# A decoder block on one core: first-pass weights as one array, row sums by products with ones, and four places reordered

## The chip, the core and the metric

The kernel runs on one core of a Trainium2 chip. TensorE (PE, with its weight loads as PEld) multiplies matrices into PSUM, VectorE (DVE), ScalarE (ACT) and GpSimd (POOL) work element by element, and SyncE (SP) issues most of the transfers. The metric is the device time of one execution in microseconds; the median of the runs is compared. Everything is computed in float32, or in float32 split into two rounded parts.

## The reference

The block works on 16 learned meta tokens followed by 1024 tokens of width 1024. Its parts, cut to what matters here:

```python
def mixer(xn, w_in, conv_a_w, conv_b_w, conv_b_bias, ln_b_gain, ln_b_bias, w_out):
    h = jnp.einsum("btd,de->bte", xn, w_in)
    b_gate, c_gate, h_a, glu_val, glu_gate = jnp.split(h, [...], axis=-1)
    y_a = b_gate * causal_depthwise_conv(c_gate * h_a, conv_a_w)
    g = glu_val * jax.nn.sigmoid(glu_gate)
    z = causal_depthwise_conv(g, conv_b_w) + conv_b_bias
    y_b = jax.nn.silu(layer_norm(z, ln_b_gain, ln_b_bias))
    return jnp.einsum("bte,ed->btd", jnp.concatenate([y_a, y_b], axis=-1), w_out)
...
h = jnp.concatenate([meta, x], axis=1)
h = h + rms_norm(mixer(rms_norm(h, pre_mix_norm), ...), post_mix_norm)
ff = swiglu(rms_norm(h, pre_ffn_norm), w_gate, w_up, w_down)
h = h + rms_norm(ff, post_ffn_norm)
return h[:, N_META:, :]
```

`rms_norm` divides by the root of the mean square of a token's row; `layer_norm` also subtracts the mean. The input projection has five groups of 512 columns: b, c, h (for the short convolution) and v, g (for the long one of 31 taps).

## The kernel before, in words

**Split products.** A float32 operand is held as a rounded high part and a low part (the rest). `mm3` (L106) then makes three products for one: high by high (L108), high by the other's low (L109), low by the other's high (L110). So every matrix operand costs a rounding on ACT and a subtraction on DVE or POOL before PE can use it.

**Order.** The program is written under a manual schedule: each engine runs its instructions in the order of the code, and an instruction that waits holds up all behind it on its engine. SP and ACT also issue transfers in that order.

**First pass (L194 to L291).** The input comes transposed, 128 features by 1040 tokens for each of eight k, the tokens cut into thirds of 348. The projection is done in units of 128 columns. Three units start together: (g,0) and (v,0) in all three thirds and (g,1) in the first third. Their weights come in pieces: `cut` (L195) splits each unit's 1024 columns into k = 0, k = 1 and 2, and the rest, so nine loads (`load_first`, L205) and nine splits (`split_first`, L208). `round_x` and `rest_x` (L182, L185) scale x by the gain of the norm, which sits in the parameter array `pr`, and split it. The norm's factor itself is put in later, as its value is known only once all of x is there: `square_x` on ACT and `add_x` on DVE sum the squares over k into `sa[0]`. At L86 to L88 six products of the identity with itself warm TensorE up; the identity is made on POOL.

**Row sums (L287 to L315).** The sum over the partitions is taken with nine narrow products, each with 128 tokens of `sa[0]` as the stationary operand and one column of `ones` (value 1/512) as the moving one (L291). The result is a small array with tokens on partitions, of which `rsqrt_n` (L119) takes the inverse root with one step of refinement. `spread_x` (L309) brings it back to one row per token on all partitions by transposes with the identity (L312) and copies into `rB`. The transposes stand between the products of unit 0, at its k = 2, 4 and 6 (`AT`, L530). `start_g` (L505) then uses `rB`.

**Units (L532 to L547).** 18 units follow, each with eight k. The accumulators come from the pool `ps1`, two tiles of three banks by turns (banks 2 to 4 and 5 to 7); the pool `aux` has banks 0 and 1. In each round the next unit's weights are split (`split_unit`, L151: ACT, then POOL, or DVE for the first), the one after is loaded, the last unit's result is worked on (`after`), and taps of the long convolution run on DVE (L372) and ACT with POOL (L358, L359). Layer norm's sums are taken within units 14 and 15: `ln_mean` (L459), `ln_var` (L472: eight narrow products) and `ln_spread` (L481: eight transposes).

**Output projection (L565 to L842).** `group` (L797) takes three, three and two blocks of 128 tokens; `OUT_BANKS` names the pairs of PSUM banks of a group's blocks. `scale_gains` (L501) multiplies two gain vectors by -0.5 on ACT.

**FFN up and gate (L844 to L1033).** The products are done with a Winograd form of Strassen's scheme on two by two blocks: for each of 11 column pairs j and both matrices m there are seven products n, numbered 1, 2, 6, 5, 7, 3, 4, each of four k. Their x side (`X[n]`: B11, B21, T2, T1, T3, B22, T4) is made once; the weight side (`a_side`, L882) is made two steps ahead: sums on DVE, rounding on ACT (L660), subtraction on DVE (L647). Step s runs over `order` (L877), which takes pairs 0 and 1 by turns and then one pair at a time. In step s come the products, then `leave` of step s-1 (L735), extra work, `a_side(s + 2)` and `split`. After a pair's last product `sums` (L782) makes four more blocks out of its result, on POOL; `split` (L771) rounds a block and writes both parts to DRAM for the down projection. `free` (L638) is the queue of PSUM banks.

**FFN down (from L1035)** runs to the end of the span and is not touched.

Of the kernel before, what the change touches and what calls it, by code (L numbers as in the profile page):

```python
# [36 lines left out]
O_MIX = 0  # L37
O_CA = O_MIX + KD
# [8 lines left out]
FILL = 40  # L47
# [8 lines left out]
def hybrid_block(ctx: ExitStack, tc: tile.TileContext, xT, x, w_in, w_out, w_gate, w_up, w_down, par, g_post, g_ffn, g_out, out):  # L56
# [17 lines left out]
    ya = ExitStack()  # L74
    yap = ya.enter_context(tc.tile_pool(name="yap", bufs=8, side="right"))
# [9 lines left out]
    make_identity(nc, ident)  # L85
    pw = aux.tile([P, 512], F32, tag="a", name="warm")  # L86
    for i in range(6):
        nc.tensor.matmul(pw[:, :P], ident, ident, start=True, stop=True)  # L88

    ones = const.tile([P, P], F32, name="ones")  # L90
    nc.vector.memset(ones, 1.0 / 512.0)
    par_ = const.tile([P, lines(NPAR)], F32, name="pr")
# [42 lines left out]
    nc.scalar.dma_start(pr, par)  # L135
# [15 lines left out]
    def split_unit(u, eng=None):  # L151
        wh, wl = (wp.tile([P, D], F32R, tag=t, name=f"{t}_{u[0]}{u[1]}") for t in ("wh", "wl"))
        nc.scalar.copy(wh, raw_w[u])
        (eng or nc.gpsimd).tensor_tensor(wl, raw_w[u], wh.bitcast(F32), op=ALU.subtract)
        split_w[u] = wh, wl
# [26 lines left out]
    def round_x(k, c=slice(None)):  # L182
        nc.scalar.activation(xh[k][:, PAD:][:, c], xs[k][:, c], AF.Copy, scale=pr[:, O_MIX + k : O_MIX + k + 1])

    def rest_x(k, c=slice(None)):  # L185
        nc.vector.scalar_tensor_tensor(xl[k][:, PAD:][:, c], xs[k][:, c], pr[:, O_MIX + k : O_MIX + k + 1], xh[k][:, PAD:][:, c].bitcast(F32), op0=ALU.mult, op1=ALU.subtract)
# [8 lines left out]
    cut = [slice(0, P), slice(P, 3 * P), slice(3 * P, D)]  # L195
    first = {}
    FIRST = [("g", 0), ("v", 0), ("g", 1)]
    for u in FIRST:
        n = f"{u[0]}{u[1]}"
        ws = wp.tile([P, D], F32, tag="ws", name=f"ws_{n}")  # L200
        wh, wl = (wp.tile([P, D], F32R, tag=t, name=f"{t}_{n}") for t in ("wh", "wl"))
        first[u] = ws, wh, wl
        split_w[u] = wh, wl

    def load_first(u, c, eng=None):  # L205
        (eng or nc.sync).dma_start(first[u][0][:, c], w_in[BASE[u[0]] + u[1]][:, c])

    def split_first(u, c):  # L208
        ws, wh, wl = first[u]
        nc.scalar.copy(wh[:, c], ws[:, c])  # L210
        nc.vector.tensor_tensor(wl[:, c], ws[:, c], wh[:, c].bitcast(F32), op=ALU.subtract)

    xs[0] = load_x(0, [third(0)])
    load_first(FIRST[0], cut[0], nc.scalar)
    load_first(FIRST[1], cut[0], nc.scalar)
    table(AF.Abs_reciprocal_sqrt)
    load_first(FIRST[2], cut[0])
    for j in (1, 2):
        nc.sync.dma_start(xs[0][:, third(j)], xT[0][:, third(j)])
    xs[1] = load_x(1)  # L220
    for u in FIRST:
        load_first(u, cut[1])
    xs[2] = load_x(2)
    for u in FIRST:
        load_first(u, cut[2])
    for k in range(3, 5):
        xs[k] = load_x(k)
    for t in xhb + xlb:
        nc.gpsimd.memset(t[:, :, :PAD].bitcast(F32), 0.0)
    sx = sm.tile([P, 16], F32, tag="sx", name="sx")  # L230
    nc.gpsimd.memset(sx, 1.0)
# [3 lines left out]
    split_first(FIRST[0], cut[0])  # L235
    round_x(0, third(0))
    rest_x(0, third(0))
    for u in FIRST[1:]:
        split_first(u, cut[0])
# [3 lines left out]
    round_x(1)  # L243
    rest_x(1)
    for u in FIRST:
        split_first(u, cut[1])
# [3 lines left out]
    for k in range(2, KD):  # L250
        round_x(k)
        rest_x(k)
        if k == 2:
            for u in FIRST:
                split_first(u, cut[2])
        square_x(k - 2)
        if k >= 4:
            add_x(k - 2)
    for k in (6, 7):
# [5 lines left out]
    def mm_k(p, w, k, t0, n, parts):  # L265
        ks = slice(k * P, (k + 1) * P)
        for j in range(parts) if isinstance(parts, int) else parts:
            ts_ = slice(t0 + j * n, t0 + (j + 1) * n)
            mm3(p[:, j, :n], w[0][:, ks], w[1][:, ks], xh[k][:, ts_], xl[k][:, ts_], k == 0, k == KD - 1)
# [1045 lines left out]
```

## Time and profile before

| | us |
|---|---|
| median of 3 runs (979.74 to 979.89) | 979.82 |
| the profiled execution's own time | 980.54 |
| its span, from the first to the last instruction | 978.8 |
| PE busy in the span | 964.4 |
| DVE busy | 726.8 |
| ACT busy | 398.1 |
| POOL busy | 274.2 |

The profile is one execution. Times in it count from the first instruction. A matmul's record is longer than the distance to the next one, since matmuls are pipelined, so the distance of the starts is what a product costs. A wait is put down to the engine whose signal came last. The first pass lies from 0 to 35 us, the units from 37 to 243, the output projection from 243 to 337, FFN up and gate from 337 on.

### The profile page before, as it was taken

The page shows a single profiled execution, that of the slowest core. Times are in us where ns is not written, and L with a number is a line of the kernel's source. Part 1 is how long each engine was busy: PE and PEld are TensorE (multiplying, and loading weights), DVE is VectorE, ACT ScalarE, POOL GpSimd, SP SyncE. Part 2 cuts the span into 40 slices and gives each one's busy share as a digit, 9 for nine tenths or more (in the row PEclk, how much of TensorE's full clock was granted, in tenths as well). Part 3 has the DMA queues.
Part 4 walks back from the last instruction along what each step waited for, and adds up shares of the span by engine and source line. Part 5 has one row for each costly group of instructions (what it writes and reads, how often), then busy time and mean ns, then how long its engine had stood idle before and what let it go on. Part 6 is the DMA issues. An engine that isn't in the chain of part 4 may idle for free.

```text
span 978.8 us, 12605 instructions
## 1 busy us (share of the span) xinstructions
PE 964.4 (99%) x4631; PEld 827.6 (85%) x4631; DVE 726.8 (74%) x1012; ACT 398.1 (41%) x657; POOL 274.2 (28%) x234
## 2 busy tenths in 40 slices
PE   8999999999999999989999999999999999999997
PEld 8999999988888878878888888888888888888885
DVE  6599999665563799999987887887877453446676
ACT  7423523154553664345333433433433333322341
POOL 0177963652000000352232231241341211112210
PEclk9999999999999999999999999999999999999999
DMA  8011111112531530436534524435309899866866
GB/s 306 23 44 44 44 44 65 65 44 87 193 134 77 193 113 1 172 151 237 207 126 141 187 114 172 154 117 203 130 33 328 308 344 381 263 190 195 318 213 240
DMA packets 59149, 156.68 MB, mean 160 GB/s; under 512 B 6224, under 2 KB 7504, under 8 KB 59088
## 3 DMA queue, kind: packets, MB, share of 16 engines
q1 hardware_dynamic: 42480, 104.02, 29.5%
q0 software_dynamic: 11088, 40.38, 12.6%
q10 hardware_dynamic: 5520, 11.48, 3.3%
q8 instruction: 36, 0.59, 0.2%
q14 instruction: 25, 0.20, 0.1%
HBM read 107.10 MB, written 48.76 MB: 159 GB/s over the span
## 4 chain that ended last, share of the span: by engine, by line
PE 81%; DVE 12%; issue 2%; ACT 2%; DMA 2%; POOL 1%; SPq 0%; ACTq 0%; DVEq 0%; POOLq 0%
PE x L110 6%; PE x L108 6%; PE x L109 6%; PE y L110 6%; PE y L109 6%; PE y L108 6%; PE qx L109 4%; PE qx L108 4%; PE qx L110 4%; PE qy L109 3%; PE qy L108 3%; PE qy L110 3%; PE po L108 2%; PE po L109 2%; PE po L110 2%; DVE ac L372 2%
## 5 line engine op out<-in xcount | busy, mean ns | idle before, releaser
L647 DVE TENSOR_TENSOR op<-u,op 128x512 fp32r<-128x512 f32 x154 | 145.1, 974 | 28.4 <-ACT op L660 27.3
L660 ACT CAST op<-u 128x512 fp32r<-128x512 f32 x154 | 91.8, 619 | 140.1 <-DVE u L647 79.3
L647 DVE TENSOR_TENSOR db<-wb,db 128x512 fp32r<-128x512 f32 x77 | 54.1, 705 | 87.7 <-ACT db L1113 85.4
L650 POOL TENSOR_TENSOR C<-C,C 128x512 f32<-128x512 f32 x11 | 17.6, 1597 | 320.6 <-ACT C L767 192.5
L1113 ACT CAST db<-wb 128x512 fp32r<-128x512 f32 x77 | 47.3, 620 | 120.8 <-PE qx L110 57.2
L108 PE MATMUL qx<-db,a 128*128 128x512 f32 x176 | 68.5, 389 | 0.0
L109 PE MATMUL qx<-db,a 128*128 128x512 f32 x176 | 68.5, 389 | 0.0
L110 PE MATMUL qx<-db,a 128*128 128x512 f32 x176 | 68.5, 389 | 0.0
L644 DVE TENSOR_TENSOR U<-y,U 128x512 f32<-128x512 f32 x66 | 43.5, 682 | 17.2 <-PE y L110 17.2
L650 POOL TENSOR_TENSOR U<-U,U 128x512 f32<-128x512 f32 x21 | 30.3, 1442 | 82.8 <-ACT U L767 55.9
L108 PE MATMUL qy<-db,a 128*128 128x512 f32 x132 | 51.3, 389 | 0.0
L109 PE MATMUL qy<-db,a 128*128 128x512 f32 x132 | 51.3, 389 | 0.0
L110 PE MATMUL qy<-db,a 128*128 128x512 f32 x132 | 51.3, 389 | 0.0
L992 POOL DMA_DIRECT2D a<-gdS x44 | 23.2, 528 | 89.9 <-PE qy L110 44.8
L372 DVE SCALAR_TENSOR_TENSOR ac<-g,pr,ac 128x512 f32<-128x512 f32 x56 | 42.1, 751 | 0.0
L372 DVE SCALAR_TENSOR_TENSOR ae<-d,pr,ae 128x512 f32<-128x512 f32 x56 | 42.1, 751 | 0.0
L647 DVE TENSOR_TENSOR u<-u,u 128x512 f32<-128x512 f32 x44 | 39.0, 906 | 0.8
L108 PEld LDWEIGHTS qx<-db,a 128*128 128x128 f32 x176 | 33.0, 188 | 6.9
L110 PEld LDWEIGHTS qx<-db,a 128*128 128x128 f32 x176 | 33.0, 188 | 6.8
L109 PEld LDWEIGHTS qx<-db,a 128*128 128x128 f32 x176 | 33.0, 188 | 6.8
L110 PE MATMUL y<-T1h,op 128*128 128x512 f32 x88 | 34.4, 390 | 1.6 <-DVE op L647 1.6
L108 PE MATMUL x<-B21h,op 128*128 128x512 f32 x88 | 34.4, 391 | 1.0 <-ACT U L739 1.0
(314 smaller groups left out, 2925.9 us busy)
## 6 DMA issues: line engine op xcount, KB each, us to landing
a<-gdS POOLq DMA_DIRECT2D x44, 512.0 KB, 4.6
a<-gdA POOLq DMA_DIRECT2D x33, 512.0 KB, 5.9
u<-w_gate_u SPq DMA_DIRECT2D x22, 512.0 KB, 5.3
u<-w_up_u SPq DMA_DIRECT2D x22, 512.0 KB, 6.2
gdS<-HI SPq DMA_DIRECT2D x44, 256.0 KB, 2.5
gdA<-HI SPq DMA_DIRECT2D x33, 256.0 KB, 2.0
gdS<-GS SPq DMA_DIRECT2D x33, 256.0 KB, 2.6
ws_o<-w_out_u SPq DMA_DIRECT2D x14, 512.0 KB, 4.9
```

What stands on the lines that cost most here:

```text
L108: nc.tensor.matmul(o, lh, rh, start=start, stop=False, skip_group_check=again)
L109: nc.tensor.matmul(o, lh, rl, start=False, stop=False, skip_group_check=again)
L110: nc.tensor.matmul(o, ll, rh, start=False, stop=stop, skip_group_check=again)
L372: nc.vector.scalar_tensor_tensor(out if i == n - 1 else acc, src[:, i : i + HALF], w(i), init if i == first else acc, op0=ALU.mult, op1=AL ...
L644: (eng or nc.vector).tensor_tensor(o, a, b, op=ALU.add)
L647: (eng or nc.vector).tensor_tensor(o, a, b, op=ALU.subtract)
L650: (eng or nc.vector).tensor_tensor(o, a, b, op=ALU.mult)
L660: nc.scalar.copy(t[:, 0, :], src)
L992: nc.gpsimd.dma_start(loads[n, j], gd[an][j])
L1113: nc.scalar.copy(t[:, 0, :], b)
```

## The change

The diff has these parts.

1. The weights of the first three units come as one array, `w_first`, k by k with the three units side by side, with the norm's gain (`mix`) in front of it. It is loaded in five pieces (k = 0, 1, 2, 3 and 4, 5 to 7), the first two on ACT's queue, and split in five pieces into two tiles `fh` and `fl`. The parameter array is loaded later, on SP. The split of the first piece's high part is on DVE. The warm-up uses `ones` and has seven products of 128 columns and one of 64.
2. In the first k, the three high-by-high products stand first, then those with the low part of x, then those with the low part of the weights. The second unit is split within the first pass.
3. The row sums are three products with `ones` as the stationary operand, which leave the sum on every partition; inverse root, refinement and scale are done there, third by third, on ACT and DVE. Their accumulators are a tile of `ps1`. The copy of `vs` is on DVE. Layer norm's sums are done in the same way, and `ln_spread` is gone.
4. `OUT_BANKS`, `free` and the banks of four turns are changed; the first two pairs of a group take other banks of the rotation.
5. The two gain vectors are scaled at the third step of the first group.
6. Product 6 of pair 0 is done in three rounds over k. In step 2 the operand's work stands ahead of T2's split.
7. The sums of pairs 0 and 1 are done on DVE, in steps 13 and 16, and the splits of steps 14 and 15 stand at the end of their steps.

```diff
-    make_identity(nc, ident)
-    pw = aux.tile([P, 512], F32, tag="a", name="warm")
-    for i in range(6):
-        nc.tensor.matmul(pw[:, :P], ident, ident, start=True, stop=True)
-
     ones = const.tile([P, P], F32, name="ones")
     nc.vector.memset(ones, 1.0 / 512.0)
+    pw = aux.tile([P, 512], F32, tag="a", name="warm")
+    for n in (P,) * 7 + (P // 2,):
+        nc.tensor.matmul(pw[:, :n], ones, ones[:, :n], start=True, stop=True)
...
-    nc.scalar.dma_start(pr, par)
...
+    CUTS = [(0, 1), (1, 2), (2, 3), (3, 5), (5, 8)]
...
+    def split_first(i, lo=True, hi=True, eng=None):
+        c = slice(CUTS[i][0] * NU, CUTS[i][1] * NU)
+        if hi:
+            (eng or nc.scalar.copy)(fh[:, c], first_raw(i))
+        if lo:
+            nc.vector.tensor_tensor(fl[:, c], first_raw(i), fh[:, c].bitcast(F32), op=ALU.subtract)
+
+    load_first(0, nc.scalar)
+    xs[0] = load_x(0, [third(j) for j in range(3)])
+    load_first(1, nc.scalar)
     table(AF.Abs_reciprocal_sqrt)
+    xs[1] = load_x(1, [third(0), slice(third(1).start, None)])
+    load_first(2)
     xs[2] = load_x(2)
+    load_first(3)
+    xs[3] = load_x(3)
+    xs[4] = load_x(4)
+    nc.sync.dma_start(pr, par)
+    load_first(4)
...
+    split_unit(UNITS[1], nc.vector)
     for k in (6, 7):
         square_x(k)
...
+    for l, r in ((0, xh), (0, xl), (1, xh)):
+        for u in FIRST:
+            o = pg1[:, :T3] if u == FIRST[2] else pu[u][:, 0, :T3]
+            nc.tensor.matmul(o, split_w[u][l][:, 0], r[0][:, :T3], start=l == 0 and r is xh, stop=False)
...
-    ss = aux.tile([P, 512], F32, tag="a", name="ss_x")
-    for i in range(NT + 1):
-        c = slice(META + i * P, META + (i + 1) * P) if i < NT else slice(0, META)
-        nc.tensor.matmul(ss[: c.stop - c.start, i : i + 1], sa[0][:, c], ones[:, :1], start=True, stop=True)
...
-    nc.scalar.copy(three(vs), pu["v", 0][:, :, :T3])
...
+    nc.vector.tensor_copy(three(vs), pu["v", 0][:, :, :T3])
+    ss = ps1.tile([P, 3, 512], F32, tag="p", name="ss_x")
...
+    for j in range(3):
+        nc.tensor.matmul(pss[j], ones, sa[0][:, third(j)], start=True, stop=True)
+    for j, c in enumerate(th):
+        nc.scalar.activation(s1x[:, c], pss[j], AF.Abs_reciprocal_sqrt, scale=512.0 / D, bias=eps[:, 0:1])
+    for j, c in enumerate(th):
+        nc.scalar.activation(s2x[:, c], s1x[:, c], AF.Square)
+        nc.vector.scalar_tensor_tensor(s2x[:, c], pss[j], 2.0 * RMS_EPS, s2x[:, c], op0=ALU.add, op1=ALU.mult)
+    for j, c in enumerate(th):
+        nc.scalar.mul(s1x[:, c], s1x[:, c], 0.5 * RSCALE)
+        nc.vector.scalar_tensor_tensor(rB[:, c], s2x[:, c], 6.0, s1x[:, c], op0=ALU.subtract, op1=ALU.mult)
...
+            nc.tensor.matmul(ln["pv"][hf], ones, ln["sq"][hf, 0], start=True, stop=True)
...
-    AT = {(0, 2): lambda: spread_x(NT, NT + 1), (0, 4): lambda: spread_x(0, 4), (0, 6): start_g, (14, 1): ln_mean, (15, 3): ln_var, (15, 7): ln_spread}
+    AT = {(0, 0): start_g, (14, 1): ln_mean, (15, 3): ln_var}
...
-    OUT_BANKS = [(2, 7), (3, 4), (5, 6)]
+    OUT_BANKS = [(5, 6), (7, 4), (2, 3)]
...
-    free = [5, 6, 3, 4, 0, 1, 2, 7]
+    free = [2, 3, 7, 4, 0, 1, 5, 6]
...
+                if n == 6 and self.j == 0:
+                    for q, (l, r) in enumerate(((0, 0), (1, 0), (0, 1))):
+                        for k in range(4):
+                            nc.tensor.matmul(p, ops[m][:, l, ks[k]], X[n][r][:, k, :], start=q == 0 and k == 0, stop=q == 2 and k == 3)
+                    continue
...
-                if m == 1 and j < NP - 1:
+                if m == 1 and 1 < j < NP - 1:
                     self.sums(nc.gpsimd)
...
-        if s == 14:
-            pairs[first_splits[s][0]].split(*first_splits[s][1:])
...
-        if s == 15:
-            pairs[first_splits[s][0]].split(*first_splits[s][1:])
         if s == 2:
-            for f in (t1_sum, t2_sum, t2_hi):
+            for f in (t1_sum, t2_sum):
                 for i in range(2, 4):
                     f(i)
             a_side(4)
-            for i in range(2, 4):
-                t2_lo(i)
+            for f in (t2_hi, t2_lo):
+                for i in range(2, 4):
+                    f(i)
...
+        if s in (13, 16):
+            pairs[s == 16].sums()
-        if s in first_splits and s not in (14, 15):
+        if s in first_splits:
             pairs[first_splits[s][0]].split(*first_splits[s][1:])
```

More of the change, by code (lines that the diff above doesn't have):

```diff
@@ L55, in hybrid_block @@
 @with_exitstack
-def hybrid_block(ctx: ExitStack, tc: tile.TileContext, xT, x, w_in, w_out, w_gate, w_up, w_down, par, g_post, g_ffn, g_out, out):
+def hybrid_block(ctx: ExitStack, tc: tile.TileContext, xT, x, w_first, w_in, w_out, w_gate, w_up, w_down, par, g_post, g_ffn, g_out, out):
     nc = tc.nc
@@ L221, in hybrid_block @@
-    for u in FIRST:
-        load_first(u, cut[1])
-    xs[2] = load_x(2)
[L224 to L227, printed above, removed]
+    NU = len(FIRST) * P
+    CUTS = [(0, 1), (1, 2), (2, 3), (3, 5), (5, 8)]
+    raw_f = [bp.tile([P, 2 * SEQ], F32, tag="x", name=f"wf{i}") for i in range(2)]
+    mix = raw_f[0][:, :KD]
+    fh, fl = (fp.tile([P, KD * NU], F32R, tag=t, name=t) for t in ("fh", "fl"))
+    for i, u in enumerate(FIRST):
+        split_w[u] = [t.rearrange("p (k c) -> p k c", k=KD)[:, :, i * P : (i + 1) * P] for t in (fh, fl)]
@@ L242, in hybrid_block @@
         rest_x(0, third(j))
[L243 to L246, printed above, removed]
+    split_first(1, lo=False)
+    for c in (third(0), slice(third(1).start, None)):
+        round_x(1, c)
+        rest_x(1, c)
+        if c == third(0):
+            split_first(1, hi=False)
     for k in range(5, KD):
@@ L307, in hybrid_block @@
     rB3 = rB.rearrange("p (a b) -> p a b", a=3)
-    def spread_x(i0, i1):
-        for i in range(i0, i1):
-            n = P if i < NT else META
-            nc.tensor.transpose(ss[:, (i - i0) * P : (i - i0) * P + n], rx[:n, i : i + 1].broadcast_to([n, P]), ident[:n, :n])
-        n = META if i0 == NT else 512
-        o = PAD if i0 == NT else PAD + META + i0 * P
-        nc.scalar.activation(rB[:, o : o + n], ss[:, :n], AF.Copy, scale=RSCALE)
+    s1x, s2x = (row(tp, "t", f"s{i}x", TT) for i in range(2))
+    th = [slice(max(j * T3, PAD), (j + 1) * T3) for j in range(3)]
+    pss = [ss[:, j, : c.stop - c.start] for j, c in enumerate(th)]
+    for j in range(3):
[8 more added lines that the diff above has]
+        nc.vector.scalar_tensor_tensor(rB[:, c], s2x[:, c], 6.0, s1x[:, c], op0=ALU.subtract, op1=ALU.mult)
+    table(AF.Sigmoid)
     gpad = {}
@@ L472, in ln_var @@
     def ln_var():
[L473 to L478 removed]
+        ln["pv"] = [aux.tile([P, 512], F32, tag="a", name=f"pv{hf}") for hf in range(2)]
+        for hf in range(2):
+            nc.tensor.matmul(ln["pv"][hf], ones, ln["sq"][hf, 0], start=True, stop=True)
+        for hf in range(2):
+            s, s2, pv = ln["sq"][hf, 1], ln["sq"][hf, 2], ln["pv"][hf]
+            nc.scalar.activation(s, pv, AF.Abs_reciprocal_sqrt, bias=eps[:, 1:2])
+            nc.scalar.activation(s2, s, AF.Square)
+            nc.vector.scalar_tensor_tensor(s2, pv, LN_EPS, s2, op0=ALU.add, op1=ALU.mult)
+            nc.vector.scalar_tensor_tensor(pv, s2, 3.0, s, op0=ALU.subtract, op1=ALU.mult)
         table(AF.Silu)
[L481 to L484 removed]
     def ln_apply():
@@ L1291, in units @@
         return w.reshape(KD, P, n, P).transpose(2, 1, 0, 3).reshape(n, P, D)
+    w_in_u = units(a["w_in"][0], 20)
+    first = np.stack([w_in_u[u].reshape(P, KD, P) for u in (16, 12, 17)], axis=2).reshape(P, -1)
     arrays = {
@@ L1295 @@
         "x_tok": x,
-        "w_in_u": units(a["w_in"][0], 20),
+        "w_first": np.concatenate([cols(a["pre_mix_norm"], KD), first], axis=1),
+        "w_in_u": w_in_u,
         "w_out_u": a["w_out"][0].reshape(KD, P, D),
```

107 lines of the change are left out of this document (40 added, 67 removed).

## The prediction

> **What bounds the kernel now.** I first read the page's busy shares and then the busy time by stretches of the span, to see where TensorE is not full.
>
> ```profile
> span 978.8 us, 12605 instructions
> PE 964.4 (99%) x4631; PEld 827.6 (85%) x4631; DVE 726.8 (74%) x1012; ACT 398.1 (41%) x657; POOL 274.2 (28%) x234
> ...
> PEclk9999999999999999999999999999999999999999
> ```
> ```profile
> 10.00:20.00 10.00, 9.87 (x60) 9.27 (x59) 7.78 (x10) 8.94 (x13) 0.00 (x0) 1.00 0.99 375
> 20.00:30.00 10.00, 10.00 (x65) 10.00 (x64) 10.00 (x10) 8.36 (x9) 0.00 (x0) 1.00 0.39 151
> ...
> 362.00:440.00 78.00, 75.40 (x331) 61.73 (x330) 74.57 (x89) 33.18 (x54) 22.49 (x14) 1.00 0.27 102
> 440.00:972.00 532.00, 531.55 (x2346) 439.95 (x2344) 381.86 (x541) 197.41 (x360) 129.54 (x135) 1.00 0.60 210
> 972.00:979.00 7.00, 0.00 (x0) 0.00 (x0) 3.62 (x9) 1.02 (x3) 0.00 (x0) 0.78 0.38 148
> ```
>
> In these stretches the columns are PE, PEld, DVE, ACT and POOL. TensorE is the bound nearly everywhere: from 440 to 972 it loses 0.45 us. A change can only pay by shortening TensorE's own list, by starting it sooner, or by removing its waits, and those waits lie before 440. The waits by engine, with PE as the filter, name them (total, times, longest):
>
> ```profile
> PE y L110 <- DVE op L647: 1.6, 1, 1.6
> ...
> PE y L109 <- DVE T2l L647: 1.0, 1, 1.0
> PE x L108 <- ACT U L739: 1.0, 1, 1.0
> PE po L108 <- DVE cv L433: 0.7, 1, 0.7
> PE p_g L108 <- ACT xh L183: 0.6, 1, 0.6
> PE p_v L108 <- ACT wh_v L210: 0.5, 1, 0.5
> PE p_c L110 <- POOL wl_c L154: 0.3, 1, 0.3
> ```
>
> Two waits belong to the start (p_g, p_v); the other five sum to 4.6 us. The sum below goes by terms: start, row sums, layer-norm sums, five waits.
>
> **The start.** The timeline of PE, with the rows that set the first pass:
>
> ```profile
> 1.37 2.93 PE L88 MATMUL warm<-ident 128*128 128x128 f32 x12 [1.37 <-POOL xh L229]
> 4.88 0.63 PE L108 MATMUL p_g<-xh,wh_g 128*128 128x348 f32 x1 [0.59 <-ACT xh L183]
> ...
> 9.12 0.49 PE L109 MATMUL p_g<-xl,wh_g 128*128 128x348 f32 x1
> 9.41 0.49 PE L110 MATMUL p_g<-xh,wl_g 128*128 128x348 f32 x1
> ...
> 10.12 0.32 PE L110 MATMUL p_v<-xh,wl_v 128*128 128x348 f32 x1
> ...
> 30.21 0.32 PE L109 MATMUL p_g<-xl,wh_g 128*128 128x348 f32 x1
> ...
> 35.28 1.97 PE L291 MATMUL ss_x<-ones,sa 128*128 128x1 f32 x18
> ```
> ```profile
> xs<-xT SPq DMA_DIRECT2D x1, 172.0 KB, 2.7
> ...
> ws_v<-w_in_u ACTq DMA_DIRECT2D x1, 64.0 KB, 4.9
> ```
> ```profile
> 0.84 0.17 DVE L91 MEMSET ones<- 128x128 f32 x1 [0.84 <-PEq L1308]
> ...
> 31.23 1.24 DVE L263 TENSOR_TENSOR sa<-sa,sa 128x1040 f32<-128x1040 f32 x1
> ...
> 40.46 1.23 DVE L154 TENSOR_TENSOR wl_v<-ws_v,wh_v 128x1024 fp32r<-128x1024 f32 x1 [1.88 <-ACT wh_v L153]
> ```
>
> At 9.12 and 9.41 two products of 348 columns start 0.29 us apart and are 0.49 long; from 10.12 on they are 0.32 long, and from 30.21 to 35.28 there are 32 of them, 0.158 apart. So TensorE runs at half rate until about 9.9, although the page's granted clock (PEclk) stands at 9 tenths or more in every slice. The first pass has 8 x 7 x 3 = 168 products, 26.5 us at 0.158, yet takes 35.28 - 4.88 = 30.4.
>
> New: the warm-up needs only the ones, set at 0.84 + 0.17 = 1.01, and is 7.5 products where six took 2.93, so 3.66 us: it fills TensorE from about 1.05 to 4.7. The first 196 KB of weights for all three units go out first on ACT's queue, where par stood. Their landing is bounded by the two rows, 2.7 and 4.9 us from issue; I take 2.7, since the 172-KB transfer is the nearest in size and row length. Issue at 0.74, rounding about 1 us: the first product at 4.5, behind the warm-up, so 4.7; at the other end 6.7. The long wait for ws_v (0.5 on PE) goes because g, v and g1 arrive together, and three products with the rounded x stand first, which covers the rest of x and of the weights.
>
> How soon the half rate ends is not in the trace for a gapless start. Before, it ended 3.0 us after the last gap (6.93 to 9.9). If the warm-up counts, 3.0 us of gapless work are over at 4.1; if the time is fixed, it stays 9.9. I take the middle, 7.0: 2.3 us at half rate lose 1.15, and the pass ends at 4.7 + 26.5 + 1.15 = 32.4 (31.2 with release by 4.7, 33.8 at 9.9).
>
> The Trainium skill, "TensorE: Matmul & The Clock Gate", Part 1, says that a gate halves the clock until one free-running window of about 3.4 us has been busy. By that page's window the release would be an estimated 6.5, 0.25 us of time better than my 7.0; the spacing rows agree with the halving, and no run here shows a gapless start.
>
> But DVE must deliver sa by then. Before, sa was ready at 31.23 + 1.24 = 32.47, 2.8 us early. The change puts the second unit's split (1.23) ahead of it on DVE and about 0.3 of extra cuts and copies, and DVE's first step comes some 0.4 earlier: 33.6 with all its idle time kept. From 10 to 20 DVE is busy 7.78 of 10, so 2.2 of that is idle, which earlier loads shorten; with it gone, 31.4. That is near the end of the pass either way. I take the middle, 32.6, for the row sums to begin: **2.7 us gained**, ends 0.5 (start 6.7, release 9.9) and 4.1. On the queues: SP gets fewer, larger loads in order of use, and par goes to its tail, which only POOL's wsum and the convolutions need; POOL then stands in that wait with the identity already made, and nothing on PE needs either.
>
> **Row sums and layer-norm sums.**
>
> ```profile
> 41.61 0.44 PE ss_x L312 x4
> ...
> 195.63 1.72 PE pm L462 x4
> 211.29 1.68 PE pst L475 x16
> ...
> 218.75 0.87 PE pv L484 x8
> ```
>
> These are rows of the chain of work. The nine narrow products (18 records) hold PE for 1.9 (the row at 35.28 has 1.97 with its drain). The two groups of four transposes cost 0.44 each and the narrow one an estimated 0.15, and behind each of four interruptions the next product starts some 0.1 late: 3.3 in all. Three products with ones over 1040 columns cost, by pm's two of 512 columns in 1.72, 1.72 x 1040/1024 = 1.75, with 0.1 behind: **1.4 gained**. The reads become fifteen element-wise steps over 348 columns, nine on ACT and six on DVE; at no more than 0.7 each (DVE has 0.68 for 512 columns, below) ACT's nine end within 6 us of the sums' end, under the 48 products of unit 0 (7.6 us); without that cover unit 1 would wait for the PSUM tile of the sums. The copy of vs moves to DVE, ahead of unit 0's first product: about 1.25 under 1.75 of sums.
>
> Layer norm: 1.68 + 0.87 + two late starts become 1.72 + one: **0.9 gained**. Its four reads per half lie under five of the unit's eight k steps.
>
> **The five waits.** A wait in that view counts from the modelled end of a matmul; T2l's shows the true loss:
>
> ```profile
> 360.28 0.39 PE L108 MATMUL y<-T2h,op 128*128 128x512 f32 x1
> 361.68 0.50 PE L109 MATMUL y<-T2l,op 128*128 128x512 f32 x1 [1.01 <-DVE T2l L647]
> 362.02 0.40 PE L110 MATMUL y<-T2h,op 128*128 128x512 f32 x1
> ```
> ```profile
> 360.34 1.29 DVE L647 TENSOR_TENSOR T2l<-T2r,T2h 128x512 fp32r<-128x512 f32 x2
> ...
> 414.37 1.66 DVE L647 TENSOR_TENSOR u<-u,u 128x512 f32<-128x512 f32 x1
> ...
> 419.35 3.48 DVE L647 TENSOR_TENSOR op<-u,op 128x512 fp32r<-128x512 f32 x2
> 424.56 0.68 DVE L647 TENSOR_TENSOR G<-G,HI 128x512 fp32r<-128x512 f32 x1
> ...
> 435.14 1.28 DVE L647 TENSOR_TENSOR op<-u,op 128x512 fp32r<-128x512 f32 x2
> ```
> ```profile
> 415.44 1.75 POOL L644 TENSOR_TENSOR GS<-U,C 128x512 f32<-128x512 f32 x1
> ```
>
> Steps of 1.40 and 0.34 replace two of 0.23, so a wait of 1.01 costs 1.28, 0.27 more than it says. Five waits: 4.6 + 5 x 0.25 = **5.8 us**.
>
> T2l (1.28): the reordered product has eight others, 8 x 0.23 = 1.8 us, before it reads T2l, so T2l is due at 362.1, and it is done at 361.63 even now. The operand's subtraction also moves ahead of T2l and no longer waits for ACT, so it lands before 360.3.
>
> U and op (1.27 and 1.85): ten DVE instructions in these two pieces of the stage take about 1.7 us where the same form takes 0.6 (0.68 alone), and all of them lie beside POOL's sums (414 to 422, 427 to 435). The sums go to DVE: 8 x 0.6 = 4.8 us there, against some 10 us of stretching, of which POOL's two remaining multiplications keep about 2. DVE and with it ACT come some 3 us earlier at both places, and splits stand behind the operand's steps instead of ahead. What is late next is the operand at the third place, with over 3 us to spare.
>
> po (0.95): the first pair of accumulators no longer takes a bank of the last unit's tile. With an extra tile in that rotation the last unit sits in banks 2 to 4, and bank 4 is now fourth: due at 243.3 + 9 x 0.23 = 245.4, free at 244.8. The other bank numbers only follow. Scaling the norm vectors two k later takes 2.1 us and a table load from before to behind two weight splits; nothing waited there, so nought.
>
> p_c (0.45): the chain to it runs through DVE's taps and POOL; they start with rB, which comes some 3 us earlier after the sums, while unit 1 starts only 1.4 earlier. The wait should go.
>
> **Sum.** 2.7 + 1.4 + 0.9 + 5.8 = 10.8. The profiled execution took 980.54 us, 1.74 over its span, and lies 0.72 above the median: 980.54 - 10.8 - 0.72 = **969.0 us**.
>
> **Rivals.**
> A, the half rate ends no sooner than before. The pass then ends at 33.8, 1.2 later than taken: 970.2. For it: the time may be set by something outside the kernel. Against: before, the work just ahead of 6.5 had two gaps. The Trainium skill's page named above calls the window free-running, so the end could move between launches by up to an estimated 3.4 us; the three times before lie within 0.15 us, which does not look so.
> B, the three waits of T2l, U and op stay, because DVE is late for its total (74.57 of 78 us busy): 4.4 back, 973.4. Against: the stretched rows.
> C, the first pass is fed no faster: ACT and DVE carry it (10.00 and 8.36 in 20 to 30), sa is late, and the start gains nothing: 971.7.
> D, slower: the sums on DVE at the stretched price, 8 x 1.74 = 13.9 us in a stage with 3.4 us of DVE left, so PE waits 10.5 more and U and op keep their 3.1: 982.6, slower from the point at which the eight cost over about 11 us. For it: nothing proves that POOL is the cause of the stretching. Against: outside POOL's work the form takes 0.6 to 0.7 throughout. At a price in between D is no change.
>
> **Chances.** Forecast 0.55 (its own range 967.5 to 970.0), A 0.16, B 0.13, C 0.10, D 0.06. The range runs from 967.2 (start at its good end) to 973.2. A measurement tells about 0.2%, 2 us, from no change: faster 0.94, within 0.03, slower 0.03, the last two from D's halves.
>
> **What would show it.** In the profile after: PE busy without a gap from about 1.1, spacing 0.158 from about 7, three products for the row sums near 32.6 with no wait for sa, no transposes in unit 0; no PE wait on T2l, U, op, cv or wl_c over 0.2; no POOL sums between 414 and 435 and 512-column subtractions at 0.6. A wait of PE for sa, or gaps before 5, would break the first term; a new wait between 400 and 440 the fourth.

## The result and the profile after

| | before | after |
|---|---|---|
| median, us (4 runs each, same chip) | 979.86 (979.74 to 980.39) | 969.40 (969.29 to 969.79) |
| ratio of the medians, 95% interval | | 0.9891 [0.9879, 0.9904] |
| span of the profiled execution, us | 978.8 | 967.6 |

The changed kernel takes 10.5 us less, faster by 1.1%; 969.0 had been forecast. The page of the changed kernel, its head and its chain of work:

```profile
span 967.6 us, 12526 instructions
...
PE 958.9 (99%) x4594; PEld 823.7 (85%) x4594; DVE 728.4 (75%) x1018; ACT 400.6 (41%) x660; POOL 260.3 (27%) x225
...
PE 99%; DMA 0%; DVE 0%; ACT 0%; issue 0%; DVEq 0%
```

The chain that ended last is TensorE alone for 99% of the span. The list of PE's waits, which had seven entries in the part quoted of before, has one (total, times, longest), and it is the 1.1 us before `ones` exists:

```profile
PE warm L88 <- DVE pr L112: 1.1, 1, 1.1
```

A list of waits says that something went, not what it was worth. The next table is worked out from the starts on PE's timeline in the two profiled executions: each row is the time from the first product of one piece of work to the first product of the next.

| from, to | before | after | gained | forecast |
|---|---|---|---|---|
| span's start to the row sums | 35.28 | 32.31 | 2.97 | 2.7 |
| row sums to unit 1 | 10.87 | 9.40 | 1.47 | 1.4 |
| unit 1 to layer norm's mean (`pm`); has the p_c wait | 149.32 | 148.83 | 0.49 | 0.45 |
| `pm` to the output projection (`po`) | 47.84 | 46.89 | 0.95 | 0.9 |
| `po` to the first product of FFN up and gate; has the po wait | 93.44 | 92.47 | 0.97 | 0.95 |
| first B11 to T2 | 23.53 | 23.53 | 0 | 0 |
| T2 (steps 4 and 5) | 12.23 | 10.88 | 1.35 | 1.28 |
| T1 to the third pair's B11 | 43.52 | 43.51 | 0.01 | 0 |
| that B11 to T3; has the waits for U and op | 24.96 | 21.79 | 3.17 | 3.12 |
| T3 to the last product | 530.17 | 530.17 | 0 | 0 |
| behind the last product's start | 7.62 | 7.77 | -0.15 | 0 |
| sum | 978.8 | 967.6 | 11.2 | 10.8 |

(The profiled executions differ by 11.2 and the medians by 10.5: the execution before that was profiled lay 0.68 above its median.)

PE's timeline of after, start and end of the first pass (start, length, instruction; a "..." leaves rows out):

```profile
1.06 3.68 PE L88 MATMUL warm<-ones 128*128 128x128 f32 x16 [1.06 <-DVE pr L112]
4.87 0.63 PE L286 MATMUL p_g<-xh,fh 128*128 128x348 f32 x1
5.29 0.43 PE L286 MATMUL p_v<-xh,fh 128*128 128x348 f32 x1
5.56 0.32 PE L286 MATMUL p_g1a<-xh,fh 128*128 128x348 f32 x1
5.72 0.32 PE L286 MATMUL p_g<-xl,fh 128*128 128x348 f32 x1
...
11.95 0.32 PE L106 MATMUL p_g<-xh,fh 128*128 128x348 f32 x1
12.37 0.40 PE L107 MATMUL p_g<-xl,fh 128*128 128x348 f32 x1
...
32.15 0.32 PE L108 MATMUL p_v<-xh,fl 128*128 128x348 f32 x1
32.31 1.92 PE L313 MATMUL ss_x<-sa,ones 128*128 128x344 f32 x6
33.81 0.58 PE L106 MATMUL p_g<-xh,fh 128*128 128x348 f32 x1
34.23 0.32 PE L107 MATMUL p_g<-xl,fh 128*128 128x348 f32 x1
```

The first product starts where it did before (4.88), but the products are 0.16 us apart from 5.56 on; before, that began at about 9.9. The clock records in the two traces say the same: the first entry, at full rate, begins at 5.51 and at 9.90. Ahead of it the record has no entry, and the views of the profile count such time as full rate, so their granted clock shows nothing of the half rate. From 11.95 to 12.37 one step is 0.42 instead of 0.16. That is a wait of 0.26 for the rest of x which the list of waits does not show, because the modelled end of the product before covers it. The three products with ones hold PE from 32.31 to 33.81, and the product behind them takes 0.42 to the next start.

DVE's timeline of after: the first pass's last sum and the copy of `vs`, then the piece in which the sums now run.

```profile
29.98 1.24 DVE L269 TENSOR_TENSOR sa<-sa,sa 128x1040 f32<-128x1040 f32 x1
32.51 1.25 DVE L303 COPY vs<-p_v 128x1044 f32<-128x1044 f32 x1 [1.29 <-PE p_v L108]
...
406.10 1.67 DVE L654 TENSOR_TENSOR u<-u,u 128x512 f32<-128x512 f32 x1
407.69 0.68 DVE L651 TENSOR_TENSOR u<-u 128x512 f32<-128x512 f32 x1
...
410.47 0.69 DVE L651 TENSOR_TENSOR GS<-U,C 128x512 f32<-128x512 f32 x1
411.20 0.69 DVE L654 TENSOR_TENSOR U<-G,U 128x512 f32<-128x512 f32 x1
411.81 0.68 DVE L654 TENSOR_TENSOR GS<-GS,G 128x512 f32<-128x512 f32 x1
412.59 0.69 DVE L654 TENSOR_TENSOR GS<-U,GS 128x512 f32<-128x512 f32 x1
```

`sa` is there at 31.22, 1.1 us ahead of the row sums. The four sums of pair 0 cost 0.69 each on DVE, where POOL took 1.75 for the first of them. One DVE instruction in this extract is still long, the 1.67 at 406.10, and POOL's timeline has its one multiplication there:

```profile
405.62 1.60 POOL L657 TENSOR_TENSOR U<-U,U 128x512 f32<-128x512 f32 x1 [2.50 <-ACT U L779]
```

POOL's instruction ends at 407.22, and DVE's at 407.77, 0.55 later: DVE's work starts about when POOL's ends. The Trainium skill, "SBUF — State Buffer", section "Who interferes with whom", says that a DVE instruction with two SBUF inputs contends with a GpSimd instruction that reads SBUF, and calls the contention over their shared port pair "an exclusive lock". These two rows agree with it: the 1.67 is 1.12 up to the end of POOL's instruction and then 0.55.

### The profile page after: what moved, and what is told of

Same layout as the page of the kernel before. It is cut to its first block, busy times and chain, and to the rows that moved or that the text cites. A ratio compares the mean times of both kernels' runs of the same rounds, so it can differ in the third digit from the quotient of the medians.

```text
span 967.6 us, 12526 instructions
## 1 busy us (share of the span) xinstructions
PE 958.9 (99%) x4594; PEld 823.7 (85%) x4594; DVE 728.4 (75%) x1018; ACT 400.6 (41%) x660; POOL 260.3 (27%) x225
## 4 chain that ended last, share of the span: by engine, by line
PE 99%; DMA 0%; DVE 0%; ACT 0%; issue 0%; DVEq 0%
PE x L108 8%; PE x L106 8%; PE x L107 8%; PE y L108 6%; PE y L106 6%; PE y L107 6%; PE qx L107 4%; PE qx L108 4%; PE qx L106 4%; PE qy L107 3%; PE qy L106 3%; PE qy L108 3%; PE po L107 3%; PE po L108 3%; PE po L106 3%; PE p_v L107 2%
## 5 line engine op out<-in xcount | busy, mean ns | idle before, releaser
L654 DVE TENSOR_TENSOR op<-u,op 128x512 fp32r<-128x512 f32 x154 | 141.8, 953 | 27.1 <-ACT op L667 25.9
L1004 POOL DMA_DIRECT2D a<-gdA x33 | 17.8, 539 | 61.3 <-PE qx L108 28.9
```

Source lines behind the costliest of these rows:

```text
L654: (eng or nc.vector).tensor_tensor(o, a, b, op=ALU.subtract)
L1004: nc.gpsimd.dma_start(loads[n, j], gd[an][j])
```

## The experiments

The theory: the gain is the sum of separate, small terms, each read off PE's starts. The rivals for each term are in the expectations. Unless a diff says otherwise an experiment is the changed kernel with one part put back. The intervals of two kernels often overlap, so what an edit costs is mostly read from the stretches of the table above, which repeat to 0.02 where an edit does not reach them (the one from the third pair's B11 to T3 only to 0.2). The layer-norm experiment is the exception, as told there.

| experiment | median, us | range | before, same chip | ratio, 95% interval |
|---|---|---|---|---|
| warm-up with the identity | 969.45 | 968.82 to 971.10 | 980.09 | 0.9896 [0.9881, 0.9911] |
| warm-up of one product | 970.56 | 970.04 to 970.66 | 980.09 | 0.9904 [0.9889, 0.9919] |
| before, with the new warm-up | 980.62 | 979.56 to 981.92 | 980.09 | 1.0009 [0.9999, 1.0019] |
| layer norm's sums as before | 980.33 | 979.83 to 980.90 | 980.09 | 1.0003 [0.9994, 1.0013] |
| sums of pairs 0 and 1 on POOL | 971.08 | 970.71 to 971.27 | 979.73 | 0.9910 [0.9894, 0.9927] |
| splits of steps 14, 15 early | 969.53 | 969.23 to 970.24 | 979.73 | 0.9896 [0.9882, 0.9911] |
| product 6 in the old order | 969.66 | 969.41 to 969.90 | 979.73 | 0.9897 [0.9882, 0.9911] |
| T2's split in the old place | 971.09 | 970.42 to 971.11 | 979.73 | 0.9910 [0.9895, 0.9924] |
| banks turned back | 970.52 | 970.44 to 970.70 | 980.18 | 0.9899 [0.9885, 0.9914] |
| row sums as before | 971.70 | 971.53 to 973.38 | 980.18 | 0.9915 [0.9900, 0.9930] |
| `FILL` of 40 | 969.71 | 969.47 to 969.97 | 980.18 | 0.9890 [0.9874, 0.9907] |
| sums in one pass | 967.87 | 967.79 to 968.24 | 980.18 | 0.9873 [0.9858, 0.9888] |

### The start: warm-up and loads

First, the changed kernel with the old warm-up (the identity, made on POOL, and six products):

```diff
-    for n in (P,) * 7 + (P // 2,):
-        nc.tensor.matmul(pw[:, :n], ones, ones[:, :n], start=True, stop=True)
+    make_identity(nc, ident)
+    for i in range(6):
+        nc.tensor.matmul(pw[:, :P], ident, ident, start=True, stop=True)
```

> The changed kernel with the old warm-up alone: six products of the identity, which POOL makes first. My theory: TensorE works up to its full rate through work without a gap, and the warm-up from 1.06 on is what let the rate go full at about 5.5 us. With the old one (about 1.4 to 4.3, then a gap of some 0.6 up to the first product at 4.9) the full rate comes later, between 7 and 9.9 us; each us at half rate costs 0.5, so 0.8 to 2.2 us more (span 968.4 to 969.8). Rival: the weights' single array made the start faster, the warm-up nothing: full rate again near 5.5, span within 0.3 of 967.6.

PE's timeline of this kernel:

```profile
4.88 0.63 PE L286 MATMUL p_g<-xh,fh 128*128 128x348 f32 x1 [0.58 <-ACT xh L181]
...
9.65 0.46 PE L108 MATMUL p_g<-xl,fh 128*128 128x348 f32 x1
9.94 0.34 PE L109 MATMUL p_g<-xh,fl 128*128 128x348 f32 x1
```

With a gap of 0.58 ahead of the first product the half rate lasts to 9.94, as it did before, and the row sums start at 33.91: 1.60 later than in the changed kernel, 1.37 sooner than before. So in this execution the new loads, splits and order of the first k alone were worth 1.4. The profiled execution took 971.1, though, and the three others 968.8 to 969.6; their starts were not seen.

Second, a warm-up of a single product of 64 columns (`for n in (P // 2,):`):

> The changed kernel with one product of 64 columns as its whole warm-up. Theory: the work that counts begins with the first product at about 4.9, full rate 3 to 7 us behind that, at 8 to 12; 1.3 to 3.3 us more than the changed kernel (span 968.9 to 970.9), less what the late start of PE leaves as slack nowhere. Rival (the instant is set from outside, by the time since the launch): full rate near 5.5 again and span within 0.3 of 967.6.

TensorE is idle for 2.85 before the first product at 4.60. The full rate comes at 8.44, 3.84 after it, and the row sums start at 33.05, 0.74 later than in the changed kernel. The median lies 1.11 above that with the identity.

Third, the other half alone: the kernel before with nothing changed but its warm-up.

```diff
+    ones = const.tile([P, P], F32, name="ones")
+    nc.vector.memset(ones, 1.0 / 512.0)
...
     pw = aux.tile([P, 512], F32, tag="a", name="warm")
-    for i in range(6):
-        nc.tensor.matmul(pw[:, :P], ident, ident, start=True, stop=True)
+    for n in (P,) * 7 + (P // 2,):
+        nc.tensor.matmul(pw[:, :n], ones, ones[:, :n], start=True, stop=True)
```

> The kernel before with the new warm-up alone (products of ones, from 1.06 to 4.7), all else as before. Theory: full rate comes earlier than the 9.9 us of before, at 5.4 to 8, although the wait for the weights of v (0.5) stays: the row sums begin 0.8 to 2.2 us sooner than at 35.28. Rival (loads and order of the first k give the whole start): the row sums begin within 0.3 of 35.28. All later terms stay, so a span of 976.5 to 978.0 by the theory and 978.5 to 978.8 by the rival.

PE's timeline of this kernel:

```profile
6.71 0.36 PE L110 MATMUL p_v<-xh,wl_v 128*128 128x348 f32 x1
6.90 0.32 PE L108 MATMUL p_g1a<-xh,wh_g 128*128 128x348 f32 x1
...
8.96 0.43 PE L109 MATMUL p_g<-xl,wh_g 128*128 128x348 f32 x1 [0.20 <-DVE xl L186]
...
10.49 0.43 PE L108 MATMUL p_g<-xh,wh_g 128*128 128x348 f32 x1 [0.46 <-ACT wh_g L210]
11.53 0.43 PE L109 MATMUL p_g<-xl,wh_g 128*128 128x348 f32 x1 [0.61 <-DVE xl L186]
```

The half rate ends at 6.7 instead of 9.9, and PE then runs into three waits that were not there: for the rest of x twice and for a weight. The row sums start at 34.96, only 0.32 sooner, and the time is that of before. A faster TensorE merely met its supply sooner. In these profiled executions the two parts pay together: 0.32 and 1.37 alone, 2.97 as a pair. The full rate came at another time in each of them, though (6.8, 9.9 and 5.6 us), so these are values of single executions.

### The row sums as they were

Nine narrow products, the transposes within unit 0, the copy of `vs` on ACT, the small tile `sx` with `FILL` at 72 to keep the later addresses, and the bank numbers that go with one tile less in `ps1`:

```diff
+    for i in range(NT + 1):
+        c = slice(META + i * P, META + (i + 1) * P) if i < NT else slice(0, META)
+        nc.tensor.matmul(ss[: c.stop - c.start, i : i + 1], sa[0][:, c], ones[:, :1], start=True, stop=True)
...
-    for j in range(3):
-        nc.tensor.matmul(pss[j], ones, sa[0][:, third(j)], start=True, stop=True)
...
-    OUT_BANKS = [(5, 6), (7, 4), (2, 3)]
+    OUT_BANKS = [(2, 3), (4, 7), (5, 6)]
```

> The changed kernel with the row sums as before (narrow products, transposes in unit 0 at k = 2, 4 and 6, vs copied on ACT), the filler kept so that later tiles lie at the changed kernel's addresses, and the banks' numbers turned back with the rotation. Theory: PE's list is 1.4 to 1.5 us longer between the sums and unit 1, and the wait for POOL's wl_c, 0.3 by the view and 0.4 to 0.5 by the starts, comes back because rB is ready some 3 us later: span 969.3 to 969.7. Rival for the second part: that wait went with the earlier start of the first pass alone, so only 1.4 to 1.5: 969.0 to 969.1.

From the row sums to unit 1 it takes 10.87 again, 1.47 more, and from unit 1 to `pm` 149.28, 0.45 more: the wait for `wl_c` is back. Its entries in PE's waits:

```profile
PE p_g L288 <- ACT xh L180: 0.8, 1, 0.8
PE p_c L108 <- POOL wl_c L151: 0.2, 1, 0.2
```

A late start is not what brings it back: in the kernel with the identity's warm-up the row sums began at 33.91, nearly as late as the 34.44 here, and unit 1 to `pm` took the 148.83 of the changed kernel. So the p_c term follows from the new row sums, whose `rB` is complete 6.45 us after they begin instead of 9.74, and is not a term by itself. The first line is something else: in this execution the first product started at 5.51, 0.64 later, and the half rate lasted to 10.29. It took 973.38, the other three 971.53 to 971.78.

### Layer norm's sums as they were

```diff
-            nc.tensor.matmul(ln["pv"][hf], ones, ln["sq"][hf, 0], start=True, stop=True)
...
+        for i in range(8):
+            nc.tensor.matmul(pst[:, i : i + 1], ln["sq"][i // 4, 0][:, i % 4 * P : (i % 4 + 1) * P], ones[:, :1], start=True, stop=True)
+        var = sm.tile([P, 16], F32, tag="var", name="var")
+        nc.vector.tensor_copy(var[:, :8], pst[:, :8])
+        ln["r"] = rsqrt_n(var[:, :8], 1.0, LN_EPS, 8, "ln")
...
+            nc.tensor.transpose(ln["pv"][i // 4][:, i % 4 * P : (i % 4 + 1) * P], ln["r"][:, i : i + 1].broadcast_to([P, P]), ident)
```

> The changed kernel with layer norm's sums as before: eight narrow products and eight transposes in place of two products with ones. Theory: PE's list is longer by 1.68 + 0.87 + a late start of 0.1 less 1.72, so 0.9 to 1.0 us more (span 968.5 to 968.6), no wait elsewhere. Rival: slack on PE in that unit hides it, within 0.2 of 967.6.

From `pm` to `po` it takes 47.76, 0.87 more, which is the term. But the kernel takes 980.33: all ten runs lie at 979.8 or more, and the whole gain is gone. It is lost where nothing was edited: `po` to the first B11 takes 93.68 (+1.2), T1 to the next B11 44.52 (+1.0), T3 to the last product 537.46 (+7.3). No wait stands in those stretches. The busy time by stretches, first of this kernel and then of the changed one (PE and its instructions, PEld, DVE, ACT, POOL, clock):

```profile
500.00:600.00 100.00, 100.00 (x433) 81.15 (x433) 78.98 (x107) 39.11 (x69) 23.06 (x15) 1.00 0.47 171
600.00:700.00 100.00, 100.00 (x434) 81.22 (x434) 80.47 (x104) 39.69 (x71) 30.55 (x20) 1.00 0.36 132
```
```profile
500.00:600.00 100.00, 100.00 (x443) 82.84 (x442) 80.70 (x107) 38.73 (x70) 24.62 (x16) 1.00 0.43 158
600.00:700.00 100.00, 100.00 (x442) 82.82 (x442) 82.49 (x107) 41.67 (x76) 28.90 (x19) 1.00 0.41 151
```

PE is busy without a gap in both, at the same clock, but gets through 433 products in 100 us instead of 442. By the starts, products of 512 columns are 231.4 ns apart on average in the FFN up and gate of this kernel and 226.7 in the changed one. The loss depends on the tile that a product reads: 226.9 for those with T2, which lose nothing, 229.2 with T1, 233.0 with T3 and 233.3 with B22, pair after pair. In FFN down, from 762 us on, the mean is 227.2. So it is no slower clock for all. What this kernel has besides the edit is the tile `var`, two times 64 bytes on each partition, which moves the tiles of the pools behind it, and one more tile in the rotation of `aux`. The diff of the change has a line that bears on this and that the prediction did not price:

```diff
-FILL = 40
+FILL = 104
```

It makes an unused tile 256 bytes larger, just what `sx` and `var` took (2 x 2 x 64), so that the later tiles stay where they were. To see whether any move does harm, the changed kernel was run with `FILL = 40`:

> The changed kernel with its filler at the old size (40 columns, 256 bytes less in each partition), nothing else. In the kernel with the old layer-norm sums a tile of 64 bytes, twice, moved all later tiles by 128 bytes, and products from the output projection on were 227 to 233 ns apart instead of 226.7, 10 us in all, with no wait. Theory: the addresses of later tiles set this, so a move by 256 bytes slows the products of the same stages too, by 2 to 25 us. Rival: it was something of that one run or of its instructions, or only odd moves matter: spacing 226.7, span within 0.2 of 967.6 (first pass aside, up to 1).

All products stay 226.7 ns apart and T3 to the last product takes 530.17. Its busy time in the same stretch:

```profile
500.00:600.00 100.00, 100.00 (x442) 82.82 (x442) 80.77 (x108) 38.78 (x69) 24.64 (x16) 1.00 0.43 158
```

This move by 256 bytes costs nothing. That the 128 bytes of `var` cost the 10 us is argued and not shown: the loss by tile fits it, but a move by 128 bytes alone, without the old layer norm, was not run.

### The sums on POOL, and what else stood in that stage

```diff
-            pairs[s == 16].sums()
+            pairs[s == 16].sums(nc.gpsimd)
```

> The changed kernel with the sums of pairs 0 and 1 on POOL again, at the changed kernel's steps 13 and 16. Theory: POOL's work beside DVE is what stretches DVE's subtractions from 0.6 to 1.7 us; eight or more of them get long again, DVE comes some 5 us later by step 17, and PE waits for U and op again: 0.5 to 3.1 us more. Rival: the places of the splits took the waits away, the engine of the sums does nothing: DVE's steps stay at 0.6 or stretch without a wait of PE, span within 0.2 of 967.6.

PE's waits, DVE's timeline and PE's timeline of this kernel:

```profile
PE x L106 <- ACT U L751: 1.2, 1, 1.2
```
```profile
407.90 1.78 DVE L651 TENSOR_TENSOR u<-u 128x512 f32<-128x512 f32 x1
409.71 1.67 DVE L654 TENSOR_TENSOR u<-u,u 128x512 f32<-128x512 f32 x1
411.30 3.48 DVE L654 TENSOR_TENSOR op<-u,op 128x512 fp32r<-128x512 f32 x2
```
```profile
418.26 0.39 PE L108 MATMUL y<-T2h,op 128*128 128x512 f32 x1
419.85 0.50 PE L106 MATMUL x<-B21h,op 128*128 128x512 f32 x1 [1.20 <-ACT U L751]
```

The 1.7-us instructions are back on DVE and the wait for U with them: 1.59 between two starts where 0.23 is usual. From B11 to T3 it takes 23.32 (+1.53), and 0.49 more is lost behind T3: 2.0 of the 3.1 that the two waits had cost. POOL is the cause of the stretching: in the kernel before, all 63 DVE subtractions and additions of this form (512 columns) in FFN up and gate that took over 1 us overlap an instruction of POOL. The rest must come from the other edits of that stage. The splits of steps 14 and 15 put back:

```diff
+        if s == 14:
+            pairs[first_splits[s][0]].split(*first_splits[s][1:])
...
-        if s in first_splits:
+        if s in first_splits and s not in (14, 15):
```

> The changed kernel with the splits of steps 14 and 15 back at their old places, ahead of the leave and of the operand's steps; the sums stay on DVE. Theory: DVE has enough time without POOL beside it, so no PE wait over 0.2 and a span within 0.2 of 967.6. Rival (the order of the splits is what helped): PE waits for U or op again, 0.5 to 3.1 us more.

The wait for U is 0.3 and the stretch takes 22.31: 0.5. Next the two parts of the T2 edit, each put back alone:

```diff
-                if n == 6 and self.j == 0:
+                if n == 6 and self.j < 0:
```

> The changed kernel with product 6 of pair 0 in its old order, so T2's low part is read by the second product; the new order of T2's split stays. Theory: with the operand's steps first T2's low part is done about as product 6 begins, so this half alone removes most of the 1.28 us: a wait of 0 to 0.3, span 967.6 to 968.0. Rival: the products' order is what does it, 0.9 to 1.3 us more.

T2 takes 11.07, 0.19 more, and no wait on `T2l` is listed. So of the 1.35 the order of the products is worth 0.2 on top of the order of the splits.

```diff
-            for f in (t1_sum, t2_sum):
+            for f in (t1_sum, t2_sum, t2_hi):
...
-            for f in (t2_hi, t2_lo):
-                for i in range(2, 4):
-                    f(i)
+            for i in range(2, 4):
+                t2_lo(i)
```

> The changed kernel with T2's split in its old place (rounding ahead of the operand's steps, low part behind them); the new order of product 6 stays. Theory: T2's low part is due eight products (1.8 us) later and was 1.3 late, so no wait is left: span within 0.2 of 967.6. Rival: the operand's low part, which is now read by the fifth product, is late in T2's place, a wait of 0.3 to 1.0.

Here T2 itself takes 10.88, as in the changed kernel: either of the two edits nearly removes that wait. But 60 us later PE's timeline has a new one:

```profile
419.18 0.39 PE L108 MATMUL y<-T2h,op 128*128 128x512 f32 x1
420.32 0.50 PE L106 MATMUL x<-B21h,op 128*128 128x512 f32 x1 [0.75 <-ACT U L751]
```

From T1 to B11 0.4 is lost and from B11 to T3 1.0, and the median is 971.09 where the kernels above with only small edits have 969.5 to 969.7 on the same chip. The stage as a whole, in the changed kernel's busy time by stretches:

```profile
352.00:430.00 78.00, 78.00 (x346) 64.55 (x345) 74.10 (x102) 35.07 (x57) 9.23 (x6) 1.00 0.28 105
```

DVE is busy for 74.10 of 78 us; a reading of this, not shown further, is that it cannot make up what it loses in step 2.

### The banks

```diff
-    OUT_BANKS = [(5, 6), (7, 4), (2, 3)]
+    OUT_BANKS = [(5, 4), (6, 7), (2, 3)]
```

with `free` and the turns to match, so that the second block's accumulator waits for the last unit's tile as before.

> The changed kernel with the old pattern of banks in the new rotation: the first block's second accumulator again takes a bank of the last unit's tile (pairs (5, 4), (6, 7), (2, 3)), the other numbers follow. Theory: PE waits for DVE's cv at its fourth product of the output projection, 0.7 by the view of waits and 0.9 to 1.0 by the starts; from that point everything is later by it (span about 968.6). Rival: the wait went because PE or DVE came at another time, not by the banks: no wait, within 0.2 of 967.6.

PE's timeline of this kernel:

```profile
237.92 0.40 PE L108 MATMUL po<-wh_o,yl 128*128 128x512 f32 x1
239.00 0.50 PE L106 MATMUL po<-wh_o,yh 128*128 128x512 f32 x1 [0.69 <-DVE cv L440]
239.34 0.39 PE L107 MATMUL po<-wl_o,yh 128*128 128x512 f32 x1
```

The steps of 1.08 and 0.34 for two of 0.23 make 0.96, and `po` to B11 takes 93.44 again, 0.97 more. The listed wait is 0.69.

### A version that is faster still

The products with ones read float32 operands, and their records come in twos (x6 for three products). Here the sums of squares are written as rounded float32, so that one pass does, for the row sums and for the variance of layer norm; the mean stays as it was. These sums are therefore less precise.

```diff
+    sr = row(gp, "g", "sr", G0 + TT, F32R)[:, G0 + PAD :]
-    nc.vector.tensor_tensor(sa[0], sa[0], sa[1], op=ALU.add)
+    nc.vector.tensor_tensor(sr, sa[0], sa[1], op=ALU.add)
...
-        nc.tensor.matmul(pss[j], ones, sa[0][:, third(j)], start=True, stop=True)
+        nc.tensor.matmul(pss[j], ones_r, sr[:, third(j)], start=True, stop=True)
...
-            nc.tensor.matmul(ln["pv"][hf], ones, ln["sq"][hf, 0], start=True, stop=True)
+            nc.tensor.matmul(ln["pv"][hf], ones_r, ln["qs"][hf], start=True, stop=True)
```

> The changed kernel with the row sums of squares and layer norm's sums of squares as one rounded pass on TensorE: the last addition writes a rounded operand, which changes that part of the computation to less precision; layer norm's mean stays as it was. Theory: PE's list alone sets the time there, and a rounded product of 512 columns takes 0.22 where these take 0.86; 1040 + 1024 columns, so 2.6 us less (span 965.0) if sa and the squares are ready as early as now; rB also comes 1.3 us sooner. Rival: DVE's sa is due too early then or unit 0 waits for the copy of vs (1.25 us against 0.45 of sums): 0.8 back, span 965.8.

PE's timeline of this kernel, and the copy of `vs` on DVE's:

```profile
32.14 0.63 PE L315 MATMUL ss_x<-sr,ones 128*128 128x344 f32 x3
33.64 0.43 PE L107 MATMUL p_g<-xh,fh 128*128 128x348 f32 x1 [0.86 <-DVE vs L305]
```
```profile
32.34 1.25 DVE L305 COPY vs<-p_v 128x1044 f32<-128x1044 f32 x1 [1.61 <-PE p_v L109]
```

`pm` to `po` takes 45.63, 1.26 less. The row sums to unit 1 gain 0.15 only, so the span is 1.4 shorter where the theory had 2.6 and the rival 1.8: the three products are short now, and unit 0 waits until `vs` has left its accumulators at 33.59, a copy that the longer sums had covered. 967.87 is the lowest median here, 1.5 below that of the changed kernel, which ran on another chip; the profiled spans differ by 1.4.

## Why the prediction was right, point by point

**The start, 2.7 forecast, 2.97 measured.** The mechanism held; two of its sizes did not, and they partly cancel. The release of the half rate was taken at 7.0 between bounds of 4.1 and 9.9 and came at 5.56, so it cost 0.4 and not 1.15. DVE was taken to deliver `sa` at 32.6 and delivered at 31.22, so it set nothing; TensorE's own list did. Against that stand a first product 0.17 later than taken and waits of 0.4 for the rest of x, which had no term. That the rest of x would be covered was right for the first k only. So it is partly luck that 2.7 and 2.97 lie this close.

**The release itself.** The prediction gave it one value. With this warm-up and no gap of more than 0.41 ahead of the first product, ten profiled executions show it between 3.96 and 6.99 by the clock record; with gaps of 0.58 (the identity's warm-up), 0.59 (before) and 0.77 there, at 9.95, 9.90 and 10.29. The Trainium skill, "TensorE: Matmul & The Clock Gate", Part 1, says that the window is free-running and that the point at which the full rate comes varies with where in it the first product lands. The trace agrees: in all fourteen profiled executions the full rate lasts a whole number of times 3.4133 us (959.14 is 281 of them, 965.97 is 283). Counted back from the release in windows of that length, TensorE's records fill 85 to 100% of the window that ends at the release and at most 83% of every one before it.

A rule that fits all fourteen is that the full rate starts at the end of the first window that is busy enough, and that each of the three gaps spoilt one window (filled to 83, 80 and 77%). Where the windows lie differs between executions, so 5.56 is one draw: by this rule the new warm-up is released between 3.96 and an estimated 7.4 (one window later), as long as no such gap follows it. The prediction held against a moving end that three times of before lay within 0.15 us. That was too small a sample: on other chips the kernel before took 978.8 to 981.9, although whether the release made that spread was not seen. Rival A was thus a matter of the execution and not only of the kernel. It came in the profiled execution of the kernel with the old row sums, whose x was late, and not in that of the changed kernel.

**Row sums and layer norm, 1.4 and 0.9 forecast, 1.47 and 0.95 measured.** Put back alone, they cost 1.47 and 0.87. The three products took 1.50 rather than 1.75, and the product behind them lost 0.26 rather than 0.1.

**The five waits, 5.8 forecast, 5.98 measured** (0.49 + 0.97 + 1.35 + 3.17). The step that carried most was reading a wait by the distances of the starts instead of its listed length. The listed 4.6 would have been 1.4 short of the 5.98. For T2l the forecast gave the credit to the order of the products; the order of the splits does nearly as much, and it is needed for what comes 60 us later.

**The rivals.** B (the three waits stay) and C (no gain at the start) did not come. D (the sums at the stretched price on DVE) fell with 0.69 for each sum, and putting the sums back on POOL brought back both the stretching and the wait. POOL's sums were rightly named as the cause of the ten long instructions; as a price they were 2.0 of the 3.1, and the splits' old places alone cost 0.5. One sum of the forecast does not come out: from the start's good end (4.1 instead of 2.7) 969.0 becomes 967.6 and not the 967.2 given as the range's low end. The 969.40 measured does not hang on it.

**What it missed.** The forecast took T3 to the last product as unchanged, and it was, to 0.01 us. But that rested on a line that had not been weighed: where `var` is put back without `FILL` being adjusted, that stretch alone is 7.3 us longer. What this says of the forecast is that a zero was given without a reason.

**What stays open.** What the warm-up by itself is worth in the changed kernel: in the profiled executions 1.6, in the medians 0.05 (969.45 against 969.40, on two chips). For the same reason the 2.97 of the start is the value of one pair of executions; the medians gained 10.46 in all against the 11.2 of the profiles. How busy a window must be, between 83 and 85% by the rule above, rests on two executions. Which moves of tiles slow the products of 512 columns. Why x came later in one execution of the kernel with the old row sums.

## What to carry to other kernels

Price a wait of TensorE by the distance of the starts around it, against the usual one: here five waits listed with 4.6 us were worth 6.0. Speed up an engine and its supply together, since in the profiled executions either alone gave 0.3 and 1.4 of the 3.0, and leave no gap between a warm-up and the first product. And on an engine that is busy for 95% of a stage, look for the price of a delay tens of microseconds further on. When a small tile is taken out or put in, keep the addresses of the large ones behind it, and compare the mean distance of products that nobody edited.

## What the runs showed of the hardware

- The same matmuls, gapless and at a granted clock of 1.00, ran 226.7 ns apart in one kernel and, depending on the tile that they read, 226.9 to 233.3 in another that differed in layer norm's sums and in 128 bytes of tiles ahead of them: 10 of 970 us.
- The half rate at the start ended between 3.96 and 10.29 us, while the profile's granted clock stood at 9 tenths or more in every slice; the distance of the starts (0.29 against 0.16 for 348 columns) and the length of the records (0.49 against 0.32) show it.
- The full rate lasted a whole number of times 3.4133 us in each of fourteen executions. The window of that length that ended at the release was filled to 85% or more, and those before it to 83% at most.
- A DVE subtraction that takes 0.69 alone took 1.67 beside one POOL multiplication of 1.60, and ended 0.55 after it.
